# Eight PSUM banks dealt out anew: three for large products, three common ones, and query-key products in a bank per head

## The chip, the cores and the metric

The kernel runs on one core of one Trainium2 chip. A core has five engines with queues of their own: PE (TensorE, the matrix products), DVE (VectorE), ACT (ScalarE), POOL (GpSimd) and SP, which here issues DMAs. Products land in PSUM, which is eight banks; a bank of 128 partitions holds 512 float32 values in each, and it can take the next product only when its last reader is done. The metric is the time of one execution on the device in microseconds (us); lower is better. Each engine works its own queue in order and stops at an instruction whose inputs or buffers aren't ready.

## The reference, cut to what matters

One inference step of two layers, 1024 prompt tokens and 8 decode tokens, width 1024. Each layer is one input projection, three groups of recurrences, gates and one output projection:

```python
p = jnp.einsum('btd,de->bte', rmsnorm(x, norm_g), w_in)      # 1024 -> 3 x 1024 and more
qa, fa, ia, za, qb, kb, vb, zb, rb, uc, zc = jnp.split(p, ...)
o_a, _ = gated_recurrence(silu(qa), k_a, ia, log_f, s_hg)    # group A: 6 heads, 64 x 64 states
o_b, _ = gated_recurrence(qb * 32**-.5, kb, vb, log_g, s_gla)# group B: 6 heads, 32 x 64 states
y_c = s5_ssm(uc, ...)                                        # group C: 16 complex recurrences
mix = concat[head_rmsnorm(o_a)*silu(za), head_rmsnorm(o_b)*silu(zb), glu(gelu(y_c))*silu(zc)]
x = x + mix @ w_out

def step(S, inp):                # gated_recurrence, one chunk of tokens
    b = jnp.cumsum(gc, axis=1)
    o_inter = jnp.einsum('bthk,bhkv->bthv', qc * jnp.exp(b), S)
    att = jnp.einsum('bthk,bshk,btshk->bths', qc, kc, decay)      # causal
    o_intra = jnp.einsum('bths,bshv->bthv', att, vc)
    S_new = jnp.exp(b_last)[..., None] * S + jnp.einsum('bshk,bshv->bhkv', kc * ..., vc)
```

The decode tokens run the same recurrences for one step from given states.

## The kernel before, in words

**Tiles.** Everything lies with features on the partitions and tokens along the rows (1032 of them: three blocks of 384, 384 and 264). The large products (`gemm_tile`: 25 column tiles of the input projection and 8 of the output projection in each layer, three blocks each) split activations and weights into a high and a low part (`hh`, `lo`, `wh`, `wl`), so a block is 24 matmuls into one bank of tag g, and DVE, ACT or POOL copy it out scaled (L742). ACT makes `wh` from the weights that came by DMA, DVE or POOL the rest `wl` (L289).

**Recurrences.** A unit of group A (`unit_a`, three per layer, two heads each) makes its decays with 16 short scans (`decay`, L874, then L881 to L884), scales keys and queries (L1014 on DVE, L985 on POOL), clamps the next ones (L977), turns the keys, and then on PE: `kv` makes v-times-k products of all 16 chunks (`v,ktm`, two aux banks), DVE scales them (L1046, two instructions) and scans them into states (`Sp`, L898); `att` makes the query-key products of 8 pairs of chunks (`qs,s`, 32 matmuls that go from head 0 to head 1 and back) into the att tile; `inter` multiplies queries and states (`qs,Sp`, into two o banks); DVE masks the att tile into `atts` in two instructions (L1078, each half of the chunks of both heads); `intra` multiplies `atts` and the values (`atts,v`, on top of `inter`'s result); `headnorm` squares the outcome, splits it (`sl` on DVE at L908, `sh` on ACT), sums it over each head with two matmuls into an aux bank and scales (L917). `unit_b` does the same for group B (`qb,kb`, `qk,kb`, masks at L1180). `decode` of the 8 new tokens runs beside it: states come by DMA, POOL updates them (L935 to L937) and SP stores them; two matmuls (`dS,qbd`) go to an aux bank.

**Group C.** `s5` makes powers of its transition in a chain of some 50 POOL steps (L362 to L367, tile `s5E`), builds matrices from it with PE and ACT (`s5PB,cbd`, `kst`), and reads outputs back from DRAM into `s5yk` (SP L636 to L645, then DVE L646). `glu` runs a gelu on ACT, with an ACT table of its own, and a product (`yh,wg`).

**What sets the order.** The Python text spawns generators and ticks them between blocks; then a scheduler of the compiler puts every engine's instructions in one fixed order from a timeline that it simulates, in which a product can start only if a bank of its tag is free. So the numbers in `psum` (L82) shape the order of all five queues, not only of PE's.

**PSUM before.** Tag g has two banks, o two, aux two; att is one tile of two banks. Every small product (states, turned keys, headnorm, decode, group C) shares aux.

Of the kernel before, what the change touches and what calls it, by code (L numbers as in the profile page):

```python
# [12 lines left out]
ALU = mybir.AluOpType  # L13

P = 128
NL = 2
T = 1024
# [21 lines left out]
def tile_hybrid_step(ctx: ExitStack, tc: tile.TileContext, a: dict, nl=NL, limit=RANGE):  # L39
    nc = tc.nc  # L40
    V, S, G, TE, SY = nc.vector, nc.scalar, nc.gpsimd, nc.tensor, nc.sync
# [38 lines left out]
        free.append(t)  # L80

    def psum(tag, shape=(P, 512), dt=F32):  # L82
        n = {"g": 2, "att": 1, "o": 2, "aux": 2}[tag]
        return ps.tile(list(shape), dt, tag=tag, bufs=n, name=nm("ps_" + tag))

    def tmp(tag, shape, dt=F32, bufs=1):
# [68 lines left out]
    def mm(out, lhsT, rhs, start=True, stop=True):  # L155
        return TE.matmul(out=out, lhsT=lhsT, rhs=rhs, start=start, stop=stop)  # L156
# [9 lines left out]
    maskA = cst.tile([P, 64], I8, name="maskA")  # L166
    maskB = cst.tile([P, P], I8, name="maskB")
# [12 lines left out]
    atts = [cst.tile([P, 2, 2, P], F32, name=f"atts{i}") for i in range(2)]  # L180
# [121 lines left out]
    def gemm_tile(i, blocks, rhs, evac, last=True, ks=range(KD), banks="ggg"):  # L302

        for b in blocks:
            o, n = BLK[b]
            p = psum(banks[b]) if isinstance(banks[b], str) else banks[b]
            for j, k in enumerate(ks):
                wh, wl = W.get(i, k)
                rh, rl = rhs(k, b)
                mm(p[:, :n], wh, rh, start=(j == 0), stop=False)  # L310
                mm(p[:, :n], wh, rl, start=False, stop=False)
                mm(p[:, :n], wl, rh, start=False, stop=(j == KD - 1))
                if j == 3:
                    tick()
                if b == blocks[-1] and last:
                    W.do_split(4 * (i + 1) + min(3, (j + 1) // 2))
            evac(b, p[:, :n])
            if b == blocks[0]:
                W.do_split(4 * (i + 1) + 1)
            tick()  # L320
# [339 lines left out]
    def layer(l, slow=False):  # L660
# [3 lines left out]
        wt = [W.push(a["wf"][l, i]) for i in range(25)]  # L664
# [14 lines left out]
        UC0, VB0, QB0, KB0, QK1, VA0, F0, Q0, ZC0, ZB0, ZA0 = 0, 2, 5, 6, 7, 8, 11, 12, 20, 17, 22  # L679
# [31 lines left out]
        if l == 0:  # L711

            late = []
            pa = psum("att", (P, 2, 512))
            gemm_tile(wt[UC0], [0, 1, 2], hrhs, lambda b, p: late.append(p), banks=("o", "o", pa[:, 0]))
            for b in range(3):
                gemm_tile(wt[UC0 + 1], [b], hrhs, lambda b, p: late.append(p), last=(b == 2), banks=("g", "g", pa[:, 1]))
                first_norm(xs, b)
                ev_uc(0)(b, late[b])
                ev_uc(1)(b, late[3 + b])  # L720
            for x in xs:
                release(x)
        else:
            for i in range(2):
                gemm_tile(wt[UC0 + i], [0, 1, 2], hrhs, ev_uc(i))
# [75 lines left out]
        for b in range(3):  # L801
            o, n = BLK[b]
            p = psum("o")
# [4 lines left out]
            t = tmp("sq", [P, 512])[:96, :n]  # L808
            x = rbT[:, o:o + n]
# [159 lines left out]
        def unit_a(j, s1, s2, qs):  # L969
# [12 lines left out]
            d = slice(T, NT)  # L982
# [35 lines left out]
            kt, qt = s2, qs  # L1018
# [3 lines left out]
            for h in range(2):  # L1022
                p = psum("aux")
                for i in range(4):
                    t0 = 512 * h + P * i
# [22 lines left out]
                states(Sp, on, 16)  # L1048


            da = [x.rearrange("p a b c -> p (a b c)").rearrange("p (h a t) -> p h a t", h=2, t=64) for x in atts]

            def att():
                p = psum("att", (P, 2, 512))
                for pair in range(8):
                    for par in range(2):
                        t0 = (2 * pair + par) * 64
                        for h in range(2):
                            mm(p[64 * par:64 * par + 64, h, pair * 64:pair * 64 + 64], kt[64 * h:64 * h + 64, t0:t0 + 64],
                               qt[64 * h:64 * h + 64, t0:t0 + 64])  # L1060
                return p

# [11 lines left out]
                                    yield x  # L1074

            def mask(p, done):
                for i, d in enumerate(da):
                    x = V.copy_predicated(out=d, mask=maskA.unsqueeze(1).unsqueeze(1).to_broadcast([P, 2, 4, 64]),  # L1078
                                          data=p[:, :, 256 * i:256 * i + 256].rearrange("p h (a t) -> p h a t", t=64))
                    behind(x, done)  # L1080

            def intra(po):

                for pair in range(8):
                    for par in range(2):
                        r = slice(64 * par, 64 * par + 64)
                        for h in range(2):
                            mm(po[par][64 * h:64 * h + 64, pair * 64:pair * 64 + 64],
                               vA[r, pair, (2 * j + h) * 64:(2 * j + h) * 64 + 64], da[pair // 4][r, h, pair % 4, :],
                               start=False, stop=(pair == 7))  # L1090

            if j == 0:
# [3 lines left out]
            p = att()  # L1096
# [13 lines left out]
            x = on[:, :T].rearrange("p (c r t) -> p r c t", r=2, t=64)  # L1110
# [6 lines left out]
        def unit_b(ti, s, q, k):  # L1117
            nh = 4 if ti == 0 else 2
            pr = nh * 32
            h0 = 4 * ti  # L1120
# [9 lines left out]
            ac, _ = yield from decay(s[:, :T], s[:, :T], pr, P, 1.0 / 16.0)  # L1130
# [34 lines left out]
            yield  # L1165
            seq = [(hp, hf) for hp in range(nh // 2) for hf in range(2)]

            def att(hp, hf):

                p = psum("att", (P, 2, 512))  # L1170
                for cc in range(4):
                    t0 = (4 * hf + cc) * P
                    for g in range(2):
                        r0 = 32 * (2 * hp + g)
                        mm(p[:, g, cc * P:cc * P + P], k[r0:r0 + 32, t0:t0 + P], q[r0:r0 + 32, t0:t0 + P])
                return p

            def mask(p):
                for i, d in enumerate(atts):
                    V.copy_predicated(out=d, mask=maskB.unsqueeze(1).unsqueeze(1).to_broadcast([P, 2, 2, P]),  # L1180
                                      data=p[:, :, 256 * i:256 * i + 256].rearrange("p h (a t) -> p h a t", a=2))

            def outputs(hp, hf, po):

                for cc in range(4):
                    c = 4 * hf + cc
                    for g in range(2):
                        hd = 2 * hp + g
                        if c:
                            mm(po[64 * g:64 * g + 64, cc * P:cc * P + P], S3[32 * hd:32 * hd + 32, c - 1, :],  # L1190
                               q[32 * hd:32 * hd + 32, c * P:c * P + P], start=(cc == 1 - hf), stop=False)
                for cc in range(4):
                    for g in range(2):
                        hd = 2 * hp + g
                        mm(po[64 * g:64 * g + 64, cc * P:cc * P + P],
                           vB[:, 4 * hf + cc, (h0 + hd) * 64:(h0 + hd) * 64 + 64], atts[cc // 2][:, g, cc % 2, :],
                           start=False, stop=(cc == 3))

            mask(att(*seq[0]))
# [19 lines left out]
        def scan_pair(f, q, k, r0, kd, head, sel, u, sfin):  # L1219

            r = slice(r0, r0 + 2 * kd)
            vx_, h0 = (vA, head) if u < 3 else (vB, head - 6)
            yield from need(3)
            on = alloc("onorm", [P, NT])
            onorm[u] = on
            kv, x = alloc("kv", [P, T]), alloc("xs", [P, T])
            po = [psum("o") for _ in range(2)]
            for v in range(64):
                p = psum("att", (P, 2, 512))
                for c in range(8):  # L1230
                    for g in range(2):
                        e = (h0 + g) * 64 + v
                        mm(p[r0 + g * kd:r0 + (g + 1) * kd, c // 4, (c % 4) * P:(c % 4 + 1) * P],
                           vx_[:, c, e:e + 1].to_broadcast([P, kd]), ident)
                V.tensor_tensor(out=kv[r], in0=k[r, :T], in1=p[r].rearrange("p a b -> p (a b)"), op=ALU.mult)
                V.tensor_tensor_scan(out=x[r], data0=f[r, :T], data1=kv[r], initial=0.0, op0=ALU.mult, op1=ALU.add)
                V.tensor_copy(out=sfin[r, v:v + 1], in_=x[r, T - 1:T])
                V.tensor_tensor(out=x[r], in0=x[r], in1=q[r, :T], op=ALU.mult)
                for h in range(2):
                    mm(po[h], sel[r, 63 - v:191 - v], x[r, 512 * h:512 * h + 512], start=(v == 0), stop=(v == 63))  # L1240
                yield
            release(kv)
            release(x)
            yield from headnorm(po[0], on[:, :512])
            yield from headnorm(po[1], on[:, 512:T])
# [383 lines left out]
```

## Time and profile before

| | |
|---|---|
| runs shown | 1069.07, 1073.71 and 1224.8 us, median 1073.71 |
| profiled execution | 1070.87 us, of which 1068.8 are its span |
| mean granted clock of TensorE | 0.972 |
| busy: PE, DVE, ACT, POOL | 94%, 60%, 46%, 44% |
| PE idle | 62.2 us of the span |

PE is the engine to watch: its idle time and the stretches at half clock are what can be won. In the timeline an instruction's idle time before it and what ended that (the releaser) stand in brackets; a wait for several things is put down to the last of them. Times in the timeline count from the span's start.

### The profile page before, as it was taken

The page shows a single profiled execution, that of the slowest core. Times are in us where ns is not written, and L with a number is a line of the kernel's source. Part 1 is how long each engine was busy: PE and PEld are TensorE (multiplying, and loading weights), DVE is VectorE, ACT ScalarE, POOL GpSimd, SP SyncE. Part 2 cuts the span into 40 slices and gives each one's busy share as a digit, 9 for nine tenths or more (in the row PEclk, how much of TensorE's full clock was granted, in tenths as well). Part 3 has the DMA queues.
Part 4 walks back from the last instruction along what each step waited for, and adds up shares of the span by engine and source line. Part 5 has one row for each costly group of instructions (what it writes and reads, how often), then busy time and mean ns, then how long its engine had stood idle before and what let it go on. Part 6 is the DMA issues. An engine that isn't in the chain of part 4 may idle for free.

```text
span 1068.8 us, 20962 instructions
## 1 busy us (share of the span) xinstructions
PE 1006.6 (94%) x8071; PEld 946.8 (89%) x8071; DVE 644.8 (60%) x1333; ACT 487.8 (46%) x1001; POOL 466.9 (44%) x668
## 2 busy tenths in 40 slices
PE   6999999999989899999999998999998989999993
PEld 5889987889889799999999997888998989999992
DVE  9985735734656766575474583393478575652345
ACT  7334124376353657634332412245563565763431
POOL 5584664114443545532172267250254363551324
PEclk9899999999989899999999999899999999999997
DMA  7131132121112021134414113112011212112314
GB/s 242 46 104 53 41 93 57 46 60 57 45 37 64 31 82 50 56 121 135 133 45 130 44 42 87 51 41 74 30 50 52 61 46 74 41 60 87 100 43 162
DMA packets 78810, 76.77 MB, mean 72 GB/s; under 512 B 24524, under 2 KB 60652, under 8 KB 78700
## 3 DMA queue, kind: packets, MB, share of 16 engines
q1 hardware_dynamic: 78700, 75.33, 23.1%
q8 instruction: 65, 1.06, 0.4%
q14 instruction: 45, 0.37, 0.1%
HBM read 58.01 MB, written 15.53 MB: 69 GB/s over the span
## 4 chain that ended last, share of the span: by engine, by line
PE 66%; DVE 12%; POOL 10%; DMA 3%; issue 3%; ACT 3%; SPq 2%; DVEq 0%; POOLq 0%; ACTq 0%
PE ps_g L156 52%; PE ps_aux L156 6%; PE ps_o L156 4%; DVE ep L874 2%; PE ps_att L156 2%; DMA dV<-vdd 1%; DMA raw<-in_wf 1%; DVE s5W L584 1%; POOL s5E L365 1%; POOL s5Bm L363 1%; POOL s5E L362 1%; POOL s5Bm L366 1%; POOL s5E L364 1%; PE ps_aux L851 1%; ACT ep L146 1%
## 5 line engine op out<-in xcount | busy, mean ns | idle before, releaser
L156 PE MATMUL ps_g<-hh,wh 128*128 128x384 f32 (+1 forms) x1168 | 384.7, 329 | 1.5 <-DVE qb L742 1.2
L156 PE MATMUL ps_g<-hh,wl 128*128 128x384 f32 (+1 forms) x1168 | 381.4, 327 | 3.5 <-POOL wl L289 3.3
L156 PE MATMUL ps_g<-lo,wh 128*128 128x384 f32 (+1 forms) x1168 | 381.5, 327 | 0.0
L156 PEld LDWEIGHTS ps_g<-hh,wl 128*128 128x128 f32 x1168 | 223.7, 192 | 7.5 <-POOL wl L289 4.3
L156 PEld LDWEIGHTS ps_g<-hh,wh 128*128 128x128 f32 x1168 | 223.6, 191 | 7.5 <-issue 2.6
L156 PEld LDWEIGHTS ps_g<-lo,wh 128*128 128x128 f32 x1168 | 223.8, 192 | 2.6 <-issue 0.8
L289 POOL TENSOR_TENSOR wl<-raw,wh 128x256 fp32r<-128x256 f32 x127 | 107.3, 845 | 262.4 <-ACT wh L146 242.2
L146 ACT ACTIVATE wh<-raw 128x256 fp32r<-128x256 f32 x258 | 102.3, 411 | 134.1 <-PE ps_g L156 115.3
L156 PE MATMUL ps_g<-m,wh 128*128 128x384 f32 (+1 forms) x567 | 136.2, 320 | 0.0
L289 DVE TENSOR_TENSOR wl<-raw,wh 128x256 fp32r<-128x256 f32 x131 | 82.3, 629 | 42.9 <-ACT wh L146 35.0
L156 PEld LDWEIGHTS ps_g<-m,wh 128*128 128x128 f32 x567 | 99.2, 188 | 0.4
L156 PE MATMUL ps_g<-m,wl 128*128 128x384 f32 (+1 forms) x261 | 83.6, 320 | 0.0
L1347 POOL TENSOR_TENSOR z<-z,sg 128x384 f32<-128x384 f32 (+1 forms) x48 | 47.2, 983 | 50.4 <-ACT sg L146 43.1
L156 PEld LDWEIGHTS ps_g<-m,wl 128*128 128x128 f32 x261 | 49.1, 188 | 0.2
L742 DVE TENSOR_TENSOR z<-ps_g,rn 128x384 f32<-128x384 f32 (+1 forms) x48 | 24.4, 509 | 27.9 <-PE ps_g L156 27.9
L146 ACT ACTIVATE sg<-z 128x384 f32<-128x384 f32 (+1 forms) x48 | 23.4, 487 | 29.7 <-DVE z L1345 29.3
L146 ACT ACTIVATE sg<-sg 128x384 f32<-128x384 f32 (+2 forms) x56 | 31.8, 569 | 5.8 <-DVE sg L779 4.8
L156 PE MATMUL ps_g<-vx,wh 128*128 128x384 f32 (+1 forms) x129 | 34.1, 322 | 0.0
L917 DVE TENSOR_TENSOR onorm<-ps_o,sq 128x512 f32<-128x512 f32 x24 | 16.5, 688 | 29.1 <-ACT sq L146 29.1
L1357 DVE SCALAR_TENSOR_TENSOR onorm<-z,vec,onorm 128x384 f32<-128x384 f32 (+1 forms) x36 | 22.0, 614 | 18.9 <-POOL z L1347 18.9
L146 ACT ACTIVATE sg<-sg,ones 128x384 f32<-128x384 f32 (+2 forms) x52 | 32.4, 623 | 0.9
L1436 DVE TENSOR_TENSOR lo<-ps_g,ext 128x384 f32<-128x384 f32 (+1 forms) x24 | 12.3, 512 | 32.9 <-PE ps_g L156 32.8
(385 smaller groups left out, 1846.0 us busy)
## 6 DMA issues: line engine op xcount, KB each, us to landing
raw<-in_wf SPq DMA_DIRECT2D x100, 256.0 KB, 2.8
raw<-in_wo SPq DMA_DIRECT2D x32, 256.0 KB, 3.2
x<-in_xT SPq DMA_DIRECT2D x16, 192.0 KB, 3.8
ext<-in_xT SPq DMA_DIRECT2D x16, 192.0 KB
x1d<-ext SPq DMA_DIRECT2D x16, 192.0 KB, 1.9
ext<-x1d SPq DMA_DIRECT2D x16, 192.0 KB, 2.3
usd<-ucp SPq DMA_DIRECT2D x4, 512.0 KB
s5U<-usd SPq DMA_DIRECT2D x32, 64.0 KB, 2.4
```

The lines of the kernel that those rows point to most:

```text
L146: return S.activation(out=out, in_=in_, func=func, **kw)
L156: return TE.matmul(out=out, lhsT=lhsT, rhs=rhs, start=start, stop=stop)
L289: e.tensor_tensor(out=wl, in0=r, in1=wh.bitcast(F32), op=ALU.subtract)
L362: e.tensor_tensor(out=dr, in0=ar, in1=br, op=ALU.mult)
L363: e.tensor_tensor(out=t, in0=ai, in1=bi, op=ALU.mult)
L364: e.tensor_tensor(out=dr, in0=dr, in1=t, op=ALU.subtract)
L742: V.tensor_tensor(out=dst[:, o:o + n], in0=p, in1=rn[:, o:o + n], op=ALU.mult)
L874: V.tensor_tensor_scan(out=g[:, cs], data0=zero[:pr].to_broadcast([pr, ch]) if plus is None else plus[:, cs], data1=x[:, cs], initial=0.0, ...
L917: V.tensor_tensor(out=dst if n < 512 else run(dst), in0=run(po), in1=run(rs), op=ALU.mult)
L1347: G.tensor_tensor(out=z[:, c], in0=z[:, c], in1=sg[:, c], op=ALU.mult)
L1357: V.scalar_tensor_tensor(out=on[:, c], in0=z[:, c], scalar=g, in1=on[:, c], op0=ALU.mult, op1=ALU.mult)
L1436: V.tensor_tensor(out=x, in0=p, in1=xo, op=ALU.add)
```

## The change

Tag g gets three banks, o keeps two, aux gets three, and the tag att is gone. A call of `att` takes two aux banks, one for each head, in place of one tile of two banks. The masks now go by head: `da[h]` and `db[g]` are whole tiles of `atts` for one head, so the two mask instructions of a unit have the same size as before (128x512) but each reads one bank, and `intra` needs both from its second matmul on (before, the first half of the chunks needed only the first). At the start of layer 0 the third block of the first tile goes to an aux bank and the second tile's blocks to three g banks; both had borrowed halves of the att tile. (The last hunk is in the body that runs only if a range check fails; it does not run here.)

```diff
     def psum(tag, shape=(P, 512), dt=F32):
-        n = {"g": 2, "att": 1, "o": 2, "aux": 2}[tag]
+        n = {"g": 3, "o": 2, "aux": 3}[tag]
...
-            pa = psum("att", (P, 2, 512))
-            gemm_tile(wt[UC0], [0, 1, 2], hrhs, lambda b, p: late.append(p), banks=("o", "o", pa[:, 0]))
+            gemm_tile(wt[UC0], [0, 1, 2], hrhs, lambda b, p: late.append(p), banks=("o", "o", "aux"))
             for b in range(3):
-                gemm_tile(wt[UC0 + 1], [b], hrhs, lambda b, p: late.append(p), last=(b == 2), banks=("g", "g", pa[:, 1]))
+                gemm_tile(wt[UC0 + 1], [b], hrhs, lambda b, p: late.append(p), last=(b == 2))
...
-            da = [x.rearrange("p a b c -> p (a b c)").rearrange("p (h a t) -> p h a t", h=2, t=64) for x in atts]
+            da = [x.rearrange("p a b c -> p (a b c)").rearrange("p (a t) -> p a t", t=64) for x in atts]

             def att():
-                p = psum("att", (P, 2, 512))
+                p = [psum("aux") for _ in range(2)]
                 for pair in range(8):
                     for par in range(2):
                         t0 = (2 * pair + par) * 64
                         for h in range(2):
-                            mm(p[64 * par:64 * par + 64, h, pair * 64:pair * 64 + 64], kt[64 * h:64 * h + 64, t0:t0 + 64],
+                            mm(p[h][64 * par:64 * par + 64, pair * 64:pair * 64 + 64], kt[64 * h:64 * h + 64, t0:t0 + 64],
                                qt[64 * h:64 * h + 64, t0:t0 + 64])
                 return p
...
             def mask(p, done):
-                for i, d in enumerate(da):
-                    x = V.copy_predicated(out=d, mask=maskA.unsqueeze(1).unsqueeze(1).to_broadcast([P, 2, 4, 64]),
-                                          data=p[:, :, 256 * i:256 * i + 256].rearrange("p h (a t) -> p h a t", t=64))
+                for h, d in enumerate(da):
+                    x = V.copy_predicated(out=d, mask=maskA.unsqueeze(1).to_broadcast([P, 8, 64]),
+                                          data=p[h].rearrange("p (a t) -> p a t", t=64))
                     behind(x, done)
...
-                               vA[r, pair, (2 * j + h) * 64:(2 * j + h) * 64 + 64], da[pair // 4][r, h, pair % 4, :],
+                               vA[r, pair, (2 * j + h) * 64:(2 * j + h) * 64 + 64], da[h][r, pair, :],
```

Group B's `att`, `mask` and `outputs` change in the same way. Every engine issues the same instructions in the same numbers, but for ACT, which loads a table 11 times before and 5 times after. The order moves. From L714 to about L1160 line numbers are one lower after.

POOL, layer 0, the first unit of group A: `qs_2942` (after: `qs_2949`) is the second unit's query tile, `dS` and `dV` are the decode of the first unit. Before:

```order
L936 TENSOR_TENSOR dV_3488<-dV_3488,k_511_3437 128x256
L937 TENSOR_TENSOR dS_3487<-dS_3487,dV_3488 128x256
L936 TENSOR_TENSOR dV_3537<-dV_3537,k_511_3437 128x256
L937 TENSOR_TENSOR dS_3536<-dS_3536,dV_3537 128x256
L985 TENSOR_TENSOR qs_2942<-qs_2942,ep_3427 128x512 x2
L893 COPY Sp_3607<-ac_3506 128x1024
```

After:

```order
L984 TENSOR_TENSOR qs_2949<-qs_2949,ep_3435 128x512 x2
L935 TENSOR_TENSOR dV_3496<-dV_3496,k_519_3445 128x256
L936 TENSOR_TENSOR dS_3495<-dS_3495,dV_3496 128x256
L892 COPY Sp_3615<-ac_3514 128x1024
L935 TENSOR_TENSOR dV_3545<-dV_3545,k_519_3445 128x256
L1010 TENSOR_TENSOR s_448_2948<-s_448_2948,s_447_2947 128x512 x2
L893 MEMSET Sp_3615 128x64
L936 TENSOR_TENSOR dS_3544<-dS_3544,dV_3545 128x256
```

The query scaling has moved ahead of the decode's four steps, of which two wait for a DMA.

SP, layer 1, group C: `ysd`, `ydd` are outputs in DRAM, `s5yk` their way back; `out_gl_out` stores a decode state. Before:

```order
L636 DMA ysd_7217<-s5Y_7153 1024x1x128
L637 DMA ydd_7218<-s5Y_7153 16x8x8
L939 DMA out_gl_out<-dS_7514 128x256
L932 DMA dV_7574<-vdd_6250 32x4x64 x3
L643 DMA s5yk_7244<-ysd_7217 16x8x128 x8
L645 DMA s5yk_7244<-ydd_7218 128x8
```

After:

```order
L636 DMA ysd_7227<-s5Y_7163 1024x1x128
L637 DMA ydd_7228<-s5Y_7163 16x8x8
L643 DMA s5yk_7254<-ysd_7227 16x8x128 x8
L645 DMA s5yk_7254<-ydd_7228 128x8
L270 DMA raw_7482<-in_wf 128x512
L270 DMA raw_7622<-in_wf 128x512
L938 DMA out_gl_out<-dS_7524 128x256
```

The read-back no longer stands behind the store of a decode state.

PE, layer 1, the first unit of group A, from the end of `kv` to the first of `inter`. Before:

```order
L156 MATMUL ps_aux_8999<-v_7679,ktm_8940 64x64 x2
L156 MATMUL ps_aux_9000<-v_7679,ktm_8940 64x64 x2
L156 MATMUL ps_att_9036<-qs_8540,s_1252_8539 64x64 x26
L156 MATMUL ps_aux_9069<-dS_8874,qbd_8870 32x64 x4
L156 MATMUL ps_aux_9069<-dS_8922,qbd_8870 32x64 x4
L156 MATMUL ps_g_9264<-hh,wh_9234 128x384
...
L156 MATMUL ps_o_9125<-qs_8540,Sp_8993 64x64 x2
```

After:

```order
L156 MATMUL ps_aux_9016<-v_7689,ktm_8956 64x64 x2
L156 MATMUL ps_aux_9052<-qs_8556,s_1268_8555 64x64 x16
L156 MATMUL ps_g_9281<-lo_129,wh_9261 128x384
...
L156 MATMUL ps_g_9369<-hh,wl_9121 128x384
L156 MATMUL ps_aux_9053<-qs_8556,s_1268_8555 64x64 x16
L156 MATMUL ps_aux_9086<-dS_8890,qbd_8886 32x64 x4
L156 MATMUL ps_aux_9086<-dS_8938,qbd_8886 32x64 x4
L156 MATMUL ps_o_9142<-qs_8556,Sp_9009 64x64 x2
```

All matmuls of head 0 now come in one run, then eight large ones, then head 1, then decode, and `inter` at once; before, 19 large ones stood between decode and `inter`. All six units of group A have this form after.

## Rows read from the trace of the kernel before

**Rows 1.** The page, part 1: busy time, share of the span, instructions.

```profile
PE 1006.6 (94%) x8071; PEld 946.8 (89%) x8071; DVE 644.8 (60%) x1333; ACT 487.8 (46%) x1001; POOL 466.9 (44%) x668
```

**Rows 2.** Waits of PE: who waited for whom, us in total, times, longest.

```profile
PE ps_aux L156 <- DVE sl L908: 10.5, 3, 5.1
...
PE ps_aux L156 <- DVE onorm L1046: 3.4, 1, 3.4
PE ps_g L156 <- POOL wl L289: 3.3, 2, 1.9
...
PE ps_o L156 <- DVE atts L1078: 2.2, 1, 2.2
...
PE ps_aux L156 <- ACT yh L146: 1.9, 1, 1.9
PE ps_o L156 <- DVE Sp L898: 1.8, 1, 1.8
...
PE ps_o L156 <- DVE atts L1180: 1.6, 1, 1.6
PE ps_g L156 <- DVE qb L742: 1.2, 1, 1.2
```

**Rows 3.** Windows: stretch, length, busy of PE to POOL, clock (PEclk), DMA.

```profile
149.10:152.50 3.40, 3.40 (x13) 3.40 (x12) 0.30 (x2) 0.52 (x2) 0.75 (x3) 0.50 0.73 177
306.10:312.90 6.80, 5.65 (x22) 5.49 (x23) 6.25 (x24) 1.92 (x4) 2.07 (x2) 0.50 0.00 0
...
400.00:560.00 160.00, 159.78 (x1010) 158.45 (x1008) 98.99 (x218) 75.97 (x180) 72.08 (x130) 1.00 0.29 90
1040.00:1069.00 29.00, 11.08 (x78) 9.77 (x77) 15.68 (x27) 5.97 (x12) 13.58 (x13) 0.74 0.43 149
```

**Rows 4.** Timeline, layer 0, first headnorm: start, us, instruction, idle before and releaser.

```profile
302.51 0.61 POOL L936 TENSOR_TENSOR dV<-dV,k 128x256 f32<-128x256 f32 x1 [4.04 <-DMA dV<-vdd]
303.89 2.48 POOL L985 TENSOR_TENSOR qs<-qs,ep 128x512 f32<-128x512 f32 x2
305.19 1.33 DVE L874 TENSOR_TENSOR_SCAN ep<-zero,s 128x64 f32<-128x64 f32 x1 [5.20 <-POOL qs L985]
307.25 0.76 PE L156 MATMUL ps_aux<-sl,obd 128*128 128x512 f32 x1 [3.64 <-DVE sl L908]
```

**Rows 5.** Timeline, layer 0, first headnorm of the second unit.

```profile
352.33 0.76 PE L156 MATMUL ps_aux<-sl,obd 128*128 128x512 f32 x1 [5.12 <-DVE sl L908]
```

**Rows 6.** Timeline, layer 1, group C.

```profile
656.51 0.36 SPq L939 DMA_DIRECT2D out_gl_out<-dS  x1
658.53 0.65 PE L156 MATMUL ps_aux<-s5PB,cbd 128*32 128x128 f32 x16 [2.06 <-ACT s5Bm L146]
665.50 0.17 DVE L646 TENSOR_TENSOR s5yk<-s5yk,yd 128x8 f32<-128x8 f32 x1 [4.61 <-DMA s5yk<-ydd]
668.75 0.79 PE L156 MATMUL ps_aux<-kst,t 16*128 16x128 f32 x2 [2.65 <-DVE kst L531]
```

**Rows 7.** Timeline, layer 1, first unit of group A.

```profile
803.97 0.98 PE L156 MATMUL ps_att<-qs,s 64*64 64x64 f32 x51
807.11 0.17 DVE L983 TENSOR_TENSOR q<-qs,ep 128x8 f32<-128x8 f32 x1 [3.47 <-ACT ep L146]
807.19 1.88 DVE L1046 TENSOR_TENSOR onorm<-ps_aux,ac 128x512 f32<-128x512 f32 x2
808.35 0.66 PE L156 MATMUL ps_aux<-dS,qbd 128*32 128x64 f32 x16 [3.41 <-DVE onorm L1046]
809.18 2.62 DVE L898 TENSOR_TENSOR_SCAN Sp<-Sp,onorm 128x1024 f32<-128x1024 f32 x1
```

**Rows 8.** Groups of PE by form, whole span: busy us, mean ns.

```profile
L156 PE MATMUL ps_o<-qs,Sp 64*64 64x64 f32 x360 | 23.2, 280 | 1.8 <-DVE Sp L898 1.8
...
L156 PE MATMUL ps_att<-qs,s 64*64 64x64 f32 x384 | 9.2, 225 | 0.0
L156 PE MATMUL ps_o<-atts,v 64*64 64x64 f32 x384 | 7.1, 222 | 2.2 <-DVE atts L1078 2.2
```

More of the change, by code (lines that the diff above doesn't have):

```diff
@@ L1166, in unit_b @@
             seq = [(hp, hf) for hp in range(nh // 2) for hf in range(2)]
+            db = [x.rearrange("p a b c -> p (a b) c") for x in atts]
             def att(hp, hf):
-                p = psum("att", (P, 2, 512))
+                p = [psum("aux") for _ in range(2)]
                 for cc in range(4):
@@ L1174, in att @@
                         r0 = 32 * (2 * hp + g)
-                        mm(p[:, g, cc * P:cc * P + P], k[r0:r0 + 32, t0:t0 + P], q[r0:r0 + 32, t0:t0 + P])
+                        mm(p[g][:, cc * P:cc * P + P], k[r0:r0 + 32, t0:t0 + P], q[r0:r0 + 32, t0:t0 + P])
                 return p
             def mask(p):
-                for i, d in enumerate(atts):
-                    V.copy_predicated(out=d, mask=maskB.unsqueeze(1).unsqueeze(1).to_broadcast([P, 2, 2, P]),
-                                      data=p[:, :, 256 * i:256 * i + 256].rearrange("p h (a t) -> p h a t", a=2))
+                for g, d in enumerate(db):
+                    V.copy_predicated(out=d, mask=maskB.unsqueeze(1).to_broadcast([P, 4, P]),
+                                      data=p[g].rearrange("p (a t) -> p a t", t=P))
             def outputs(hp, hf, po):
@@ L1195, in outputs @@
                         mm(po[64 * g:64 * g + 64, cc * P:cc * P + P],
-                           vB[:, 4 * hf + cc, (h0 + hd) * 64:(h0 + hd) * 64 + 64], atts[cc // 2][:, g, cc % 2, :],
+                           vB[:, 4 * hf + cc, (h0 + hd) * 64:(h0 + hd) * 64 + 64], db[g][:, cc, :],
                            start=False, stop=(cc == 3))
@@ L1228, in scan_pair @@
             for v in range(64):
-                p = psum("att", (P, 2, 512))
+                p = [psum("aux") for _ in range(2)]
                 for c in range(8):
@@ L1232, in scan_pair @@
                         e = (h0 + g) * 64 + v
-                        mm(p[r0 + g * kd:r0 + (g + 1) * kd, c // 4, (c % 4) * P:(c % 4 + 1) * P],
+                        mm(p[c // 4][r0 + g * kd:r0 + (g + 1) * kd, (c % 4) * P:(c % 4 + 1) * P],
                            vx_[:, c, e:e + 1].to_broadcast([P, kd]), ident)
-                V.tensor_tensor(out=kv[r], in0=k[r, :T], in1=p[r].rearrange("p a b -> p (a b)"), op=ALU.mult)
+                for h in range(2):
+                    c = slice(512 * h, 512 * h + 512)
+                    V.tensor_tensor(out=kv[r, c], in0=k[r, c], in1=p[h][r], op=ALU.mult)
                 V.tensor_tensor_scan(out=x[r], data0=f[r, :T], data1=kv[r], initial=0.0, op0=ALU.mult, op1=ALU.add)
```

## The prediction

> **What bounds the kernel now.** I read the page first: PE is busy for 1006.6 of 1068.8 us [rows 1], so no other engine sets the time, and what can be won is PE's 62.2 us of idle time, what half clock costs, and nothing else unless the matmuls themselves change. Next I cut the span into windows: from 400 to 560 PE is busy for 159.78 of 160 us at full clock, and the tail from 1040 for 11.08 of 29 [rows 3]. The stretches that are full can't give anything. The start and the tail idle on chains that the order leaves as they were. So the losses that the change can touch lie between 140 and 360 us (layer 0's recurrences) and between 620 and 880 (layer 1's). Then I read PE's waits there [rows 2]: the longest are for `sl` of headnorm, 10.5 us in three waits, then a dozen of 1 to 4 us each. Last, the clock in windows: behind most waits of over 1.6 us lies a stretch in which the granted clock is 0.50, the lower of its two levels, 1.2 GHz in place of 2.4. There are eight of these between start and tail: five last 3.4 us, as at 149.1, and three some 6.8 us, as at 306.1 [rows 3]. Work in them goes at half speed, so a stretch costs half its length, 1.7 or 3.4 us. A wait is therefore priced with the stretch that follows it.
>
> **What the waits of before cost.** Wait and half-clock loss, place by place:
>
> - Headnorm, layer 0, first unit: 3.64 + 3.4 = 7.0. DVE stood 5.20 us at a decay scan that waited for POOL's scaling (L985); POOL had stood 4.04 us at a decode step for its DMA, ahead of it in the queue [rows 4].
> - The same in the second unit: 5.12 + 3.4 = 8.5 [rows 5].
> - Group C, layer 1: 2.06 + 2.65 + 3.4 = 8.1. The first is a product without an aux bank until ACT had emptied one; the second comes from DVE, which stood 4.61 us for `s5yk`'s DMA, which SP could issue only after a store of decode states at 656.51 [rows 6].
> - Layer 1, first unit: 3.41 + 1.7 = 5.1. A decode product waits for the aux bank of `kv`; DVE would have emptied it, but stood 3.47 us at L983 for ACT [rows 7].
> - Layer 1, second unit: masks 2.2, `sl` 10.5 - 3.64 - 5.12 = 1.7, and 1.7 of clock = 5.6 [rows 2].
> - `Sp` 1.8 + 1.7 = 3.5; group B's masks 1.6 + 1.7 = 3.3; `yh` 1.9; `wl` 3.3 + 1.7 = 5.0; `qb` 1.2 [rows 2].
>
> The sum is 49.2 us.
>
> **What is left of them.** In the new order POOL's L984 stands ahead of the decode steps, and DVE's decay scans ahead of `sl` are done earlier against PE; I leave 0.7 and 1.0 us for the two headnorms. The read-back of `s5yk` no longer waits for a store, and a third aux bank takes the s5 product; POOL's chain of powers now runs without other work in between, so weights that POOL splits come right behind it: 1.5 left. In layer 1's first unit L982 still stands ahead of `kv`'s product, with the same ACT chain; PE has more work to cover it, but not all: 2.0 + 1.7 of clock. The second unit's masks have moved ahead of a product and a gate step, its scans have not moved: 3.0. Group B's masks 0.5, `yh` 0 (six table loads less ahead of it on ACT), `wl` half, 2.5, as nothing in the change speaks to it, `qb` 0 with a third g bank. That is 0.7 + 1.0 + 1.5 + 3.7 + 3.0 + 0.5 + 2.5 = 12.9. Below nothing none of these can go; above, each can stay whole.
>
> **What the change adds.** Three things.
>
> *The wait of `inter` for `Sp`.* The chain from the end of `v,ktm` is two products and a scan: from 807.19 to 811.80, 4.6 us [rows 7]. Ahead of `inter`, PE now has head 0's 16 matmuls, 8 large ones, head 1's and decode. A large matmul takes about 160 / 1010 = 0.16 us [rows 3], decode 0.66 [rows 7]; a matmul leaves two records, so a head is 32 records. With 37 ns each (below) that is 1.2 + 1.3 + 1.2 + 0.66 = 4.3: a wait of 0.3, in six units 2 us. With 24 ns it is 3.5, a wait of 1.1, 6.6 us in all. Ends 0 and 6.6, I take 2.
>
> *Query-key matmuls by head.* Before, head 0 and head 1 alternate: 9.2 us for 384 records, 24 ns each [rows 8]. After, a run of 16 stays with one head's 64 rows and changes only its output half. No row shows that pattern. Nearest are `atts,v`, which changes rows every second matmul (7.1 / 384 = 18.5 ns), and `qs,Sp`, which uses two of the four 64x64 parts in turn (23.2 / 360 = 64 ns) [rows 8]. Half the array in turn at `atts,v`'s rate would be 37 ns; I take that: (37 - 24) x 384 = 5.0 us. Ends: 0, and (64 - 24) x 384 = 15.5. The two unknowns work against each other: quicker matmuls make a longer wait for `Sp`.
>
> The Trainium skill has a rule that speaks against this edit: in "TensorE: Matmul & The Clock Gate", Part 3, what overlaps and what doesn't, a weight load overlaps running matmuls only if it goes to other rows of the array. By that rule `att` by head takes the upper end, and `atts,v`'s 18.5 ns, with pairs on the same rows, is only half in agreement.
>
> *Waits that the new order makes elsewhere.* All five queues are reordered. What this costs shows in no row before; a stall here is typically 1.8 us, and about every second has a short half-clock stretch behind it, so 2.7. I allow three, 8.1 us; none and six are the ends.
>
> The masks cost what they did (two of the same size). That `intra` needs both instead of one from its second matmul on is covered where large products stand between; if these are used up, a wait of one mask follows.
>
> **Sum.** 49.2 - 12.9 - 2 - 5.0 - 8.1 = 21.2 us less. The profiled execution took 1070.87 us (its span 1068.8 and 2.1 around it), 0.3% under the median 1073.71. So 1070.9 - 21 = **1050 us**. That is 2.2% under the median; 2%, about what a measurement of this kernel can tell from no change, lies at 1052.2 and 1095.2.
>
> **Rivals.**
>
> 1. *The stalls move.* Each queue is in order, and most waits above came from DVE, POOL or ACT standing at something; take one away and the next item in the queue may be late. For it: layer 1's second unit, where masks, `sl` and DVE's scans are late by turns. Against: in three of the large places the cause itself is out of the way in the new order. With half of the 49.2 back and the additions: 1070.9 - 24.6 + 15.1 = 1061.
> 2. *Matmuls of one head run one behind the other,* at `qs,Sp`'s 64 ns: 15.5 instead of 5.0, and no wait for `Sp`: 1050 + 10.5 - 2 = 1058. The rule of the Trainium skill on rows, named above, would have it so.
> 3. *The banks were not the limit.* Only 1.2 us of waits went to a copy out of a g bank [rows 2], so a third one has little to give. If the order's other gains don't hold, what goes is group C's 8.1 and `qb`'s 1.2, what comes is 5.0: 1067. The Trainium skill's "TensorE: Matmul & The Clock Gate", in "HAM oscillation — how this bites in real kernels", reports a kernel that gained nothing further from a second set of PSUM banks; by that the time would be about the same as before.
> 4. *Slower: too few common banks.* `kv` holds two of three aux banks, head 0 takes the third, and head 1 must wait until DVE has multiplied the first bank out. If DVE stands there as in layer 1's first unit, that costs 3.41 + 1.7 = 5.1 [rows 7] in each of six units, 25.6 more than now. It decides where the first product of `kv` begins over 1.2 + 1.3 = 2.5 us behind `v,ktm`. With no gains elsewhere and 5.0 for the heads: 1070.9 + 25.6 + 5.0 = 1101. Against it: of PE's waits for that product the trace shows one in six units [rows 2].
>
> **Chances.** The forecast 0.50 (1036 to 1058), rival 1 0.21, rival 2 0.12, rival 3 0.08, rival 4 0.09. Range 1035 to 1071: it holds the forecast, rivals 1 to 3, and leaves out most of rival 4. Two thirds of the forecast lie under 1052.2, a quarter of rival 2 and a fifth of rival 1: faster 0.33 + 0.03 + 0.04 = 0.40. Two thirds of rival 4 lie over 1095.2: slower 0.06. Within 2%: 0.54.
>
> **What will show it.** PE's wait for `sl` should fall from 10.5 us to under 3, and the half-clock stretches between start and tail from eight to about four. `s5yk` should land within 10 us of its issue and PE's wait for `kst` be gone. The group `qs,s` tells rival 2 from the forecast: 9.2 us before, about 14 by the forecast, 25 by rival 2. Rival 4 shows as waits of `qs,s` for `onorm` at L1045. If PE's idle time falls by over 20 us and the time doesn't, the matmuls are slower than I took them; if the idle time stays near 62, rival 1 or 3 is right.

## The result and the profile after

The changed kernel takes 1052.97 us (median of four runs, 1049.4 to 1056.13); the kernel before, run beside it, 1071.57. The ratio of the fast runs, which leaves out the one of 1224.8 us, is 0.9824, with a 95% interval of 0.9804 to 0.9844: 1.8% faster, where 2.2% was forecast (1050 us). The profiled execution took 1056.13 us, the slowest of the four, and its span 1054.2; so the traces differ by less than the medians.

The page, part 1, of the kernel after:

```profile
PE 994.6 (94%) x8071; PEld 940.2 (89%) x8071; DVE 649.4 (62%) x1333; ACT 479.2 (45%) x995; POOL 472.2 (45%) x668
```

PE is idle for 1054.2 - 994.6 = 59.6 us, against 62.2 [rows 1]. So the time did not come out of PE's idle time as the page shows it: PE is *busy* for 12 us less, with the same 8071 matmuls. Who PE waits for did change:

```profile
PE ps_o L156 <- DVE Sp L897: 8.6, 6, 2.3
...
PE ps_g L156 <- POOL wl L289: 4.5, 6, 1.3
PE ps_aux L156 <- DVE sl L907: 4.2, 4, 2.4
PE ps_aux L156 <- DVE onorm L1045: 3.8, 2, 2.1
PE ps_aux L850 <- DVE atts L1181: 3.1, 2, 1.9
...
PE ps_aux L156 <- DVE bm L879: 1.8, 1, 1.8
```

The wait for `sl` fell from 10.5 to 4.2 us, those for `kst`, `s5Bm`, `yh`, `qb` and A's masks [rows 2, 6] are gone. In their place stand `inter`'s wait for `Sp` in all six units (8.6, before 1.8), head 1's for the bank of `kv`'s product (3.8), and that of transposes (L850) for an aux bank which a mask of group B has yet to empty (3.1). The wait for `wl` rose, from 3.3 to 4.5.

Three of the half-clock stretches, and a full one, in windows (columns as in [rows 3]):

```profile
82.70:86.10 3.40, 3.40 (x18) 2.81 (x18) 3.11 (x9) 2.98 (x9) 1.78 (x4) 0.50 0.01 1
...
366.00:376.20 10.20, 7.96 (x72) 7.44 (x73) 4.94 (x8) 2.41 (x6) 2.54 (x4) 0.50 0.12 29
871.20:878.00 6.80, 5.11 (x69) 4.60 (x66) 2.51 (x3) 0.46 (x2) 0.28 (x1) 0.50 0.05 8
400.00:560.00 160.00, 158.90 (x1008) 157.80 (x1007) 96.06 (x211) 70.81 (x169) 72.41 (x132) 1.00 0.32 98
```

There are still eight of them between start and tail, 41 us long in all against 37.5 before. About four were forecast.

Groups of PE by form, after:

```profile
L156 PE MATMUL ps_o<-qs,Sp 64*64 64x64 f32 x360 | 23.4, 301 | 8.6 <-DVE Sp L897 8.6
...
L156 PE MATMUL ps_aux<-s5V,s5O 64*128 64x136 f32 x128 | 13.6, 292 | 0.5 <-DVE s5O L609 0.5
L156 PE MATMUL ps_aux<-qs,s 64*64 64x64 f32 x384 | 13.5, 220 | 3.8 <-DVE onorm L1045 3.8
...
L156 PE MATMUL ps_aux<-v,ktm 64*64 64x64 f32 x384 | 7.0, 221 | 0.0
```

and two of the same groups before:

```profile
L156 PE MATMUL ps_aux<-s5V,s5O 64*128 64x136 f32 x128 | 17.1, 292 | 0.1
...
L156 PE MATMUL ps_aux<-v,ktm 64*64 64x64 f32 x384 | 10.0, 222 | 0.0
```

`qs,s` grew by 4.3 us, from 24 to 35 ns a record [rows 8]; `v,ktm` and `s5V,s5O` fell by 3.0 and 3.5.

**Where the time went.** I split the time of each trace from PE's first instruction to its last: each matmul gets the time from its start to the next one's. Pauses of over 0.06 us count as waits; what a matmul in a half-clock stretch takes beyond the mean of its kind at full clock is the clock's cost; the rest is work at full clock. The start, ahead of the clock's first record, counts as half clock. How a kind is cut (by tiles and shape, or more finely) moves the clock column, and with it the work, by up to 1.6 us; the waits do not depend on it. "Changes" counts the places, at full clock and without a pause, at which PE goes from large products (into g banks and their like) to small ones or back. Each row is one execution. The versions are those of the experiments below; of the last two only waits and changes are given.

| version | median us | waits | clock | work | changes |
|---|---|---|---|---|---|
| before | 1071.57 | 43.2 | 21.0 | 985.7 | 370 |
| after | 1052.97 | 38.6 | 16.3 | 978.4 | 301 |
| split alone (old banks) | 1080.15 | 50.8 | 19.9 | 988.3 | 375 |
| g 2, aux 4 | 1054.06 | 47.7 | 17.6 | 968.3 | 304 |
| after, heads alternate | 1047.32 | 35.3 | 16.5 | 973.6 | 303 |
| before, POOL edges | 1070.72 | 44.2 | 20.3 | 986.4 | 367 |
| after, kv by bank | 1062.02 | 43.5 | 15.5 | 981.5 | 295 |
| before, shifted | 1089.17 | 63.4 | 23.7 | 978.4 | 330 |
| before, shifted 2 | 1076.46 | 53.2 | 22.0 | 980.5 | 355 |
| after, shifted | 1058.92 | 36.9 | 16.8 | 983.9 | 315 |
| after, shifted 2 | 1064.49 | 47.0 | 15.7 | 981.0 | 319 |
| heads alternate, decode later | 1046.06 | 38.5 | | | 310 |
| g 2, aux 4, products ahead of `inter` | 1053.34 | 47.5 | | | 317 |

Of the 16.6 us between the first two, waits give 4.6, the clock 4.7 and work at full clock 7.3. (The span differs by 14.6: the last store of this execution landed some 2 us later.) The number of changes does not set the work: 330 of them go with 978.4 us in one version, 315 with 983.9 in another.

### The profile page after: what moved, and what is told of

The parts are those of the page before. It is cut to its first block, busy times and chain, and to the rows that moved or that the text cites. A ratio compares the mean times of both kernels' runs of the same rounds, so it can differ in the third digit from the quotient of the medians.

```text
span 1054.2 us, 20947 instructions
## 1 busy us (share of the span) xinstructions
PE 994.6 (94%) x8071; PEld 940.2 (89%) x8071; DVE 649.4 (62%) x1333; ACT 479.2 (45%) x995; POOL 472.2 (45%) x668
## 4 chain that ended last, share of the span: by engine, by line
PE 68%; DVE 15%; POOL 7%; ACT 3%; issue 3%; DMA 2%; SPq 1%; DVEq 0%; POOLq 0%; ACTq 0%
PE ps_g L156 54%; PE ps_aux L156 8%; PE ps_o L156 5%; DVE s5W L584 1%; DVE Sp L897 1%; ACT ep L146 1%; DVE ep L873 1%; PE ps_aux L850 1%; POOL wl L289 1%; DVE onorm L1045 1%; DMA x<-in_xT 1%; ACT sg L146 1%; DVE wl L289 1%; DVE sl L907 1%; POOL s5E L364 1%
## 5 line engine op out<-in xcount | busy, mean ns | idle before, releaser
L289 POOL TENSOR_TENSOR wl<-raw,wh 128x256 fp32r<-128x256 f32 x127 | 109.6, 865 | 219.9 <-ACT wh L146 207.0
L741 DVE TENSOR_TENSOR z<-ps_g,rn 128x384 f32<-128x384 f32 (+1 forms) x48 | 24.4, 509 | 32.8 <-PE ps_g L156 32.7
L156 PE MATMUL ps_o<-qs,Sp 64*64 64x64 f32 x360 | 23.4, 301 | 8.6 <-DVE Sp L897 8.6
L156 PEld LDWEIGHTS ps_o<-qs,Sp 64*64 64x64 f32 x360 | 21.2, 199 | 10.8 <-DVE Sp L897 9.6
```

Source lines behind the costliest of these rows:

```text
L289: e.tensor_tensor(out=wl, in0=r, in1=wh.bitcast(F32), op=ALU.subtract)
L741: V.tensor_tensor(out=dst[:, o:o + n], in0=p, in1=rn[:, o:o + n], op=ALU.mult)
```

## The experiments

Theory: the common banks let the scheduler set the queues so that PE waits less and small products come in whole runs; the third g bank does little; query-key matmuls of one head cost more than alternating ones. Against it stood, in turn, that the split by head is itself the gain, that the third g bank is, that any new order does as well, and that each stall taken away comes back elsewhere.

**1. The split alone,** with the banks of before.

```diff
-        n = {"g": 3, "o": 2, "aux": 3}[tag]
+        n = {"g": 2, "att": 2, "o": 2, "aux": 2}[tag]
...
-                p = [psum("aux") for _ in range(2)]
+                p = [psum("att") for _ in range(2)]
```

> The kernel with the split by head alone: g 2 banks, o 2, aux 2 as before, and query-key products in two single banks of a tag of their own. On PE, DVE, POOL and SP nearly everything stands as before the change. If the gain comes from the order that the freed banks allow (my theory), this one stays within 0.5% of before, 1066 to 1075 us, with POOL's scaling again behind the decode steps and PE's wait for sl near 10 us. If splitting by head were itself the gain (masks and products that need one bank only), it would come out near 1055. The group qs,s should stay at 9 to 10 us, since heads still alternate.

Measured: 1080.15 us, ratio 1.0079 (1.0054 to 1.0104), `sl` 9.1 us in four waits, `qs,s` 8.8. The gain isn't in the split: the old waits are there. It is even 0.8% slower, over the range I gave; waits rose by 7.6 us, among them those for `Sp` (6.2, before 1.8) and for copies out of g banks (L741: 8.0 in all for `s`, `qb` and `z`, before 1.4):

```profile
PE ps_aux L156 <- DVE sl L907: 9.1, 4, 5.1
PE ps_o L156 <- DVE Sp L897: 6.2, 3, 4.2
...
PE ps_g L156 <- DVE s L741: 3.3, 1, 3.3
```

**2. The third g bank undone,** a fourth common one in its place.

```diff
-        n = {"g": 3, "o": 2, "aux": 3}[tag]
+        n = {"g": 2, "o": 2, "aux": 4}[tag]
...
```

> The change with g at 2 banks and aux at 4: the third bank for large products undone, a fourth common one in its place. My theory (a third g bank has little to give, PE waited 1.2 us for copies out of g; common banks make the order): 1046 to 1058 us, PE's waits of qs,s for onorm (3.8 us) gone, qs,s back at 9 us since both heads have a bank and alternate, and 1 to 3 us of waits for g copies back. Rival, the third g bank is the gain: 1063 to 1072, with waits for copies out of g above 8 us.

Measured: 1054.06 us, ratio 0.9844 (0.9815 to 0.9873), as the change within its interval. Waits for copies out of g came back with 3.6 us, over the 1 to 3 expected; `qs,s` ran alternating at 6.7 us:

```profile
L156 PE MATMUL ps_aux<-v,ktm 64*64 64x64 f32 x384 | 7.0, 221 | 0.0
L156 PE MATMUL ps_aux<-qs,s 64*64 64x64 f32 x384 | 6.7, 218 | 0.0
```

So common banks carry the gain, and a third g bank isn't needed for it; whether the eighth bank is a third g or a fourth aux makes no difference to the time. That doesn't say that a third g bank is worth nothing, for two things moved at once: against the change this version has 9.1 us more of waits (`sl` 8.6, a g copy 3.1) and 10.1 us less of work, the least in the table, of which `qs,s` gives 6.8. `qs,s` no longer waits for `onorm`, but decode does (5.2).

**3. Heads alternate again,** by order edges between the matmuls of `att`, in the changed kernel.

```diff
                         for h in range(2):
-                            mm(p[h][64 * par:64 * par + 64, ...
+                            x = mm(p[h][64 * par:64 * par + 64, ...
+                            if pair + par + h:
+                                after(x, last)      # order only, no semaphore
+                            last = x
```

> The changed kernel with one thing added: an order edge between query-key matmuls, so that head 0 and head 1 alternate as before the change; some 22 large matmuls then lie between v,ktm and them, in place of 8 in the middle. My theory: qs,s falls from 13.5 to about 9 us, PE's wait of inter for Sp from 8.6 to under 3 and that of qs,s for onorm from 3.8 to under 2: 4.5 + 5.6 + 1.8 = 12 us, of which half may come back elsewhere: 1040 to 1049 us. Rival (the waits only move to the next late thing, masks and headnorm): 1050 to 1056.

Measured: 1047.32 us, ratio to before 0.9774 (0.9748 to 0.9801). The two waits and the group moved as expected, and a new wait of 9.7 us came: a turn of decode's product on PE that now stands within `inter` and waits for ACT.

```profile
PE ps_aux L953 <- ACT dV L146: 9.7, 4, 4.0
...
PE ps_o L156 <- DVE Sp L901: 2.7, 2, 2.0
...
PE ps_aux L156 <- DVE onorm L1049: 1.1, 1, 1.1
```

```profile
L156 PE MATMUL ps_aux<-qs,s 64*64 64x64 f32 x384 | 8.6, 221 | 1.1 <-DVE onorm L1049 1.1
```

Work fell by 4.8 us, waits by 3.3. It is 0.5% under the change.

**4. POOL's order alone,** in the kernel before: edges hold the decode's multiplications behind the scaling of the next queries.

```diff
-                G.tensor_tensor(out=vb, in0=vb, in1=k8[...], op=ALU.mult)
+                x = G.tensor_tensor(out=vb, in0=vb, in1=k8[...], op=ALU.mult)
+                for y in scaled:                    # the scaling traced last
+                    after(x, y)
```

> The kernel before, banks untouched, with order edges that put POOL's scaling of the next query tile ahead of the decode's multiplications (L936 in the kernel before), as the change's order has it. My theory (layer 0's two headnorm stalls, 7.0 and 8.5 us, come from that place in POOL's queue): PE's wait for sl falls from 10.5 to 2 to 5 us and the time by 6 to 13 us, to 1058 to 1065. Rival (DVE's in-order queue, not POOL's, makes sl late: scans and gate steps ahead of it): sl stays above 8 us and the time at 1068 to 1075.

Measured: 1070.72 us, ratio 0.9987 (0.997 to 1.0004). My theory got its mechanism and not its gain: the wait for `sl` fell from 10.5 to 4.2, and others of 1.7 and 3.1 us came up within 10 us of the old places.

```profile
PE ps_aux L156 <- DVE sl L914: 4.2, 4, 1.6
...
PE ps_g L156 <- DVE z L748: 3.1, 1, 3.1
...
PE ps_att L156 <- DVE qs L1022: 1.7, 1, 1.7
```

DVE is the engine behind all of them; that its own work in that stretch isn't done sooner when POOL's is would explain it, but no run isolates it. The sum of waits is 44.2, before 43.2.

**5. `v,ktm` one bank after the other,** in the changed kernel.

```diff
                 for c in range(16):
-                    pr_, par = divmod(c, 2)
+                    par, pr_ = divmod(c, 8)
```

> The changed kernel with the 32 v,ktm matmuls of a unit written bank by bank: 16 that read one half of the rows, then 16 that read the other, in place of changing halves every second matmul. My theory (runs that stay on one half of the rows overlap less; that is what made qs,s go from 9.2 to 13.5 us in the change and v,ktm from 10.0 to 7.0): the group v,ktm rises from 7.0 to 12 to 14 us. Since the first bank is full earlier, DVE's product starts earlier and PE's waits for onorm and Sp (12.4 us together) fall, so the time moves less than that, 1049 to 1058 us. Rival (a run costs the same in any order of rows, and v,ktm fell only because qs,s no longer stands between): v,ktm stays at 7 to 8 us, and the time falls to 1044 to 1050.

Measured: 1062.02 us, ratio to before 0.9895 (0.9861 to 0.993), 9 us over the change and 4 over the range I gave. The group `v,ktm`:

```profile
L156 PE MATMUL ps_aux<-qs,s 64*64 64x64 f32 x384 | 12.3, 232 | 4.5 <-DVE onorm L1045 4.2
L156 PE MATMUL ps_aux<-v,ktm 64*64 64x64 f32 x384 | 11.5, 221 | 0.0
```

From 7.0 to 11.5 us, 18 to 30 ns a record, with almost nothing else in between (the last few of a unit alternate with the first `qs,s`): a run on one half of the rows is slower. But such a run also stays in one PSUM bank, here as in `att` by head, and the quick orders change both; which of the two costs the time, no run here separates. The waits didn't fall as expected (`Sp` 7.6, `onorm` 4.2); on the whole they rose by 4.9.

**6, 7. Another draw of the order.** One idle turn more in a thread of group C (PU 2 for 1), in the kernel before and after.

> The kernel before with one idle turn more in group C's thread (PU 2 in place of 1): nothing of the work or the banks changes, but the compiler's scheduler deals out all queues anew. My theory (the banks make the gain): 1063 to 1080 us, and 360 to 380 changes on PE between large and small products, as before. Rival (any new order does as well, and the one before was an unlucky draw): under 1058.

> The changed kernel with the same idle turn more. My theory: 1044 to 1062 us, with some 300 changes on PE between large and small products. Rival (the change's order was a lucky draw): over 1063.

**8, 9. A second draw** (PT 5 for 4).

> The kernel before with another idle turn in group C's thread (PT 5 in place of 4), a second new draw of the order with the old banks. My theory (banks): 1063 to 1092 us. Rival (draw of the order): under 1058.

> The changed kernel with the same (PT 5 in place of 4). My theory (banks): 1044 to 1062 us. Rival (draw of the order): over 1063.

Measured: with the old banks 1089.17 and 1076.46 us, ratios to before 1.0151 (1.0111 to 1.0191) and 1.0062 (1.0038 to 1.0087); with the new ones 1058.92 and 1064.49, ratios 0.9875 (0.9832 to 0.9918) and 0.9947 (0.9929 to 0.9964). Two of the four lie outside the ranges I gave: 1089.17 is 9.2 us over its own, and 1064.49 is 2.5 us over and thus where I had put the rival, that the change's order was a lucky draw. The first shifted one has 330 changes on PE, fewer than I expected. A neutral shift moves the time by up to 18 us, about as much as the change did. Still all three pairs go the same way, by 18.6, 30.3 and 12.0 us, and the slowest draw with the new banks is faster than the fastest with the old. So in these three draws the order bears on the size of the gain and not on its side. In these pairs waits and clock together go from 64.2, 87.1 and 75.2 to 54.9, 53.7 and 62.7 us; work goes from 985.7, 978.4 and 980.5 to 978.4, 983.9 and 981.0. So what the banks give in every draw is less of waits and clock, by 9.3, 33.4 and 12.5 us. The work falls by 7.3 in the first pair and rises by 5.5 and 0.5 in the others, so that fall comes with the draw. Constant in the work are `v,ktm`, 3 us less with the new banks, and `qs,s`, 4 to 6 more.

**10. Decode's turn later,** in the version of experiment 3.

```diff
             act(out=stg, in_=po[:, :P], func=AF.Copy)
+            yield from pause(4)
             po = psum("aux")
             TE.transpose(out=po[:, :P], in_=stg, identity=ident)
```

> The alternating version (1047.3 us) with four idle turns in the decode between the copy of its product and the product's turn on PE, so that this no longer stands in the middle of inter, where PE waited 9.7 us in four places for ACT's copy of dV. My theory: that wait falls under 1.5 us, and with it two or three half-clock stretches; most of these lie on qs,Sp and cost little. 1047.3 - 8 - 1 = 1038, range 1035 to 1044. Rival (PE's waits move to masks, headnorm and Sp, as with the POOL edges): 1045 to 1050.

Measured: 1046.06 us, ratio to before 0.9758 (0.9722 to 0.9794), the fastest version, 0.1% under experiment 3 and not to be told from it. The rival was right: the 9.7 us are gone, masks and headnorm took their place, and waits went from 35.3 to 38.5 us.

```profile
PE ps_o L156 <- DVE atts L1085: 8.0, 6, 3.0
PE ps_aux L156 <- DVE sl L911: 6.5, 7, 2.6
...
PE ps_o L156 <- DVE Sp L901: 3.7, 3, 2.0
```

**11. Large products ahead of `inter`,** in the version with g 2 and aux 4: four idle turns more between `att` and `inter`, and `inter`'s first product held in the place in the order that the program text gives it.

> The version with g 2 and aux 4 (1054.1 us, the least matmul time at full clock of all versions so far, but 7.8 us of waits of inter for Sp and DVE) with four idle turns more in a unit between the query-key products and inter, so that some 23 large matmuls come to stand between them. My theory: inter's waits fall from 7.8 to under 3 us and the short matmuls (qs,s and v,ktm under 7.5 us each) stay: 1054 - 5 - 2 = 1047, range 1041 to 1051. Rival (waits only move, as in the two trials before with order edges): 1051 to 1058.

Measured: 1053.34 us, ratio to before 0.9846 (0.9827 to 0.9865), no gain over 1054.06. `inter` still waits for `Sp`, once for 5.2 us, now that DVE comes to it later:

```profile
PE ps_aux L156 <- DVE sl L907: 8.5, 5, 3.1
PE ps_o L156 <- DVE Sp L897: 8.2, 5, 5.2
...
PE ps_aux L156 <- DVE onorm L1045: 5.1, 4, 2.8
```

## Why the prediction was right, and where not

The time, 1050 against 1052.97, and the side were right. The sum under it was not right in all its terms, and two errors, of 17 and 12 us, for the most part cancelled: waits and clock fell by 9.3 us where it had 26, and work at full clock fell by 7.3 where it rose by 5.0. That the time came out within 3 us is therefore luck: the other two draws of the order gave 30.3 and 12.0 us in place of 18.6.

- **The waits of before** went much as the sum had them: `sl` to 4.2 (under 3 was said; 2.41 of it at the first headnorm, where 0.7 was left), `kst` and `s5Bm` to nothing; only `wl` rose where the sum halved it. The read-back of `s5yk` no longer stands behind a decode store; from the first store's issue at 634.94 it took 9.5 us to DVE (under 10 was said):

```profile
634.94 0.60 SPq L636 DMA_DIRECT2D ysd<-s5Y  x1
...
642.12 0.43 SPq L645 DMA_DIRECT2D s5yk<-ydd  x1
```

```profile
644.48 0.44 DVE L646 TENSOR_TENSOR s5yk<-s5yk,yd 128x8 f32<-128x8 f32 x1 [4.78 <-DMA s5yk<-ydd]
```

- **What fails is the allowance for new waits,** 2 us for `inter` and 8.1 elsewhere. The cover was sized well, and so was the bare chain to `Sp`: in layer 0's first unit it takes 4.3 us from the end of `v,ktm` to the scan's end, for 4.6 estimated, and `inter` waits 0.50. What the sum left out is that DVE, which works both links of the chain, need not be free: in the other units the chain takes 4.8 to 8.0 us. Timeline of layer 0's second unit after, PE:

```profile
319.35 1.16 PE L156 MATMUL ps_aux<-v,ktm 64*64 64x64 f32 x64
320.33 1.10 PE L156 MATMUL ps_aux<-qs,s 64*64 64x64 f32 x32
...
322.96 1.15 PE L156 MATMUL ps_aux<-qs,s 64*64 64x64 f32 x32
324.04 0.43 PE L156 MATMUL ps_aux<-dS,qbd 128*32 128x64 f32 x16
326.75 1.43 PE L156 MATMUL ps_o<-qs,Sp 64*64 64x64 f32 x22 [2.27 <-DVE Sp L897]
```

and DVE:

```profile
320.55 1.95 DVE L1045 TENSOR_TENSOR onorm<-ps_aux,ac 128x512 f32<-128x512 f32 x2 [0.41 <-PE ps_aux L156]
323.23 0.17 DVE L982 TENSOR_TENSOR q<-qs,ep 128x8 f32<-128x8 f32 x1 [0.73 <-ACT ep L146]
323.31 3.38 DVE L897 TENSOR_TENSOR_SCAN Sp<-Sp,onorm 128x1024 f32<-128x1024 f32 x1
```

From the end of `v,ktm` at 320.5, PE has 4.0 us of other work, to 324.47; 4.3 was the estimate. But DVE stops 0.73 us between product and scan for a small step of the decode that needs ACT, and the scan takes 3.38 us. In both layers' third units DVE comes to the product 3 to 4 us after `v,ktm`'s end, so that head 1 waits too. Layer 0, PE and then DVE:

```profile
358.94 1.16 PE L156 MATMUL ps_aux<-v,ktm 64*64 64x64 f32 x64
...
364.23 1.15 PE L156 MATMUL ps_aux<-qs,s 64*64 64x64 f32 x32 [1.62 <-DVE onorm L1045]
```

```profile
363.16 1.89 DVE L1045 TENSOR_TENSOR onorm<-ps_aux,ac 128x512 f32<-128x512 f32 x2
```

  This is rival 4's mechanism, the last aux bank held until DVE's product, in two units of six and with 1.6 and 2.1 us in place of 5.1 in each.

- **By the test that the prediction set itself,** idle time that stays near 62 us means rival 1 or 3. In this pair it was rival 1, the stalls move, and experiments 4, 10 and 11 show how: a wait taken away is mostly followed by the next thing that DVE is late with. That 1053 and not rival 1's 1061 came out is due to the work at full clock, below.

- **Half the length of a half-clock stretch** was too high a price. Eight stretches stayed, and they lie elsewhere: five of them, 27 of the 41 us, on `qs,Sp`, which the wait for `Sp` precedes. At full clock, timeline after:

```profile
284.75 2.86 PE L156 MATMUL ps_o<-qs,Sp 64*64 64x64 f32 x46 [0.50 <-DVE Sp L897]
...
872.95 2.25 PE L156 MATMUL ps_o<-qs,Sp 64*64 64x64 f32 x36 [1.69 <-DVE Sp L897]
```

The second lies in the stretch from 871.2 at 0.50, the first at full clock: 62 ns a record in both. A large product does take twice the time, 0.32 us from start to start against 0.17 (before, in and outside a stretch):

```profile
308.56 0.52 PE L156 MATMUL ps_g<-lo,wh 128*128 128x384 f32 x1
308.88 0.52 PE L156 MATMUL ps_g<-hh,wl 128*128 128x384 f32 x1
```

```profile
301.00 0.34 PE L156 MATMUL ps_g<-lo,wh 128*128 128x384 f32 x1
301.17 0.34 PE L156 MATMUL ps_g<-hh,wl 128*128 128x384 f32 x1
```

Of 360 records of `qs,Sp`, 224 ran at half clock after, 50 before. The whole clock's cost between start and tail was 13.2 us for 37.5 us of stretches before and 11.3 for 41 after, about a third of the length and less. The rest of the clock's 4.7 us lies in start and tail, which the prediction had left alone.

- **Query-key matmuls by head** were sized right: 13.5 us, 35 ns a record, for 14 and 37. Rival 2 (25 us) is out. Experiment 5 shows much the same price, 18 to 30 ns, for staying on one half of the rows in `v,ktm`. The Trainium skill ("TensorE: Matmul & The Clock Gate", Part 3, what overlaps and what doesn't) says that a weight load overlaps running matmuls only if it goes to other rows. That points the right way here, though not to the upper end that the prediction read out of it (13.5 us, not 25), and the runs that stay on their rows stay in their bank too. The price isn't as high as `qs,Sp`'s 62 to 65 ns, which alternates rows and is slow nonetheless; by that rule it would be quick, and why it isn't no run here tells.

- **Work that falls** had no term at all, and it is a matter of the draw (experiments 6 to 9). `v,ktm` had been cut in pieces or mixed with `qs,s` when only two aux banks were there, and in all versions with three or four, but for experiment 5, it takes 7.0 to 7.4 us. `s5V,s5O`'s 3.5 us went with this draw: 12.5 us in the shifted kernel with the old banks, 17.1 in the shifted one with the new.

- **The third g bank** was said to have little to give. Experiment 2 shows that the gain comes without it, with a fourth aux bank in its place; what it gives by itself stays open, as no run has two g banks and three aux. Rival 3, that the banks were not the limit, is out by the three draws.

## What to carry to other kernels

A dealing-out of PSUM banks acts through the whole order: price the waits that it removes, but allow for as many new ones as the engine behind them (here DVE) is late with, and try two or three neutral shifts of the order before believing a per cent. Count small matmuls by their pattern too: whole runs of `qs,s` and `v,ktm` that change rows and bank every matmul or every second one were 1.6 to 2 times as quick as runs that stay on one half of the rows and in one bank. A half-clock stretch is priced by what lies in it.

## What was not expected of the hardware

`qs,Sp` runs at 62 ns a record at either clock level, so the lower clock cost nothing there. Whether going from large to small products or back has a price is not settled: over the traces the large matmul ahead of a change took 199 ns on the mean, for 161 in a run of large ones, but the medians, 177 and 174, hardly differ. For small ones ahead of a large one the kind decides: a transpose of values (`ident,vf`) took 30 ns to the large one's start for 115 in its own run, `qs,s` 148 for 20. A shift of the order that adds no work moved the time by up to 1.5%.
